# A bidirectional encoder layer on one core: the four later conditioning rows, from TensorE matmuls in one sweep to VectorE sums over two

## The chip, the cores and the metric

One core of one Trainium2 chip runs the whole kernel in one launch. The metric is the device time of that launch in microseconds (us), taken from its first to its last instruction with what the launch itself adds; lower is better. Before the change the median of three runs is 2424.1 us (2421.89 to 2425.3).

The core has five instruction streams that run beside each other and wait for each other by semaphores: PE (TensorE, matmuls, with its weight loads shown apart as PEld), DVE (VectorE), ACT (ScalarE), POOL (GpSimd) and SP (SyncE, which here issues nearly all DMA transfers). [...]

## The reference

One layer of an encoder (D_MODEL = 1024), run for a prompt of 2048 rows and for a sample of 256 rows, each with a conditioning vector `c` of its own. Cut to what matters here:

```python
def encoder_layer(x, c, ...):
    mod = silu(c) @ ada_w + ada_b                       # (1024) @ (1024 x 6144)
    sh1, sc1, gt1, sh2, sc2, gt2 = split(mod, 6)        # six rows of 1024
    h = rmsnorm(x, norm_mix) * (1 + sc1) + sh1
    x = x + gt1 * hybrid_mixer(h, w_in, w_fnet, w_out)  # FNet half and retention half
    h = rmsnorm(x, norm_mlp) * (1 + sc2) + sh2
    x = x + gt2 * (square(relu(h @ w_mlp_in)) @ w_mlp_out)
    return x
```

`mod` has one row for each of the two sequences. `sh1` and `sc1` are wanted before the first projection; `gt1`, `sh2`, `sc2` and `gt2`, the later rows of the title, are wanted only behind the mixer, in the output projection and the MLP.

## The kernel before, in words

The 2304 rows are 18 tiles of 128 rows (16 prompt, 2 sample). The program has these stages: a start in which `ada0` makes `sh1` and `sc1`; a pass over all tiles that projects the Fourier part and forms the first butterflies on DVE (to about 165 us); the **first sweep** over the tiles from the last to the first, which makes keys and values (`w_k`, `w_v`) and the backward retention states, and runs the rest of the Fourier transform (`dft`, `pa`, `pb`, `fs`) in small jobs between (about 165 to 470 us); the **second sweep** in forward order, which makes queries and the gate (`w_q`, `w_g`), and the retention itself (about 470 to 775 us); then the output projection and the MLP, the other two thirds of the time.

Matrices are multiplied in float32r as three products of a high and a low part, so each projection of one tile is 24 matmuls 128x512 (`proj<-whi,hhi`, `proj<-wlo,hhi`, `proj<-whi,hlo`, eight each). The matmuls of the conditioning rows are plain float32, and the profile shows each of them as two records, one for each pass.

The order of instructions on every engine is fixed when the program is built: a scheduler plays the program through on a timeline of its own and writes each engine's list. Tiles come from pools of a fixed number of slots, and an instruction that makes a new tile waits until a slot is free. Those that matter here: `S` has 13 slots of 128x1024 float32 (inputs `h`, their parts `hhi` and `hlo`, `kv`, `qkT`, the weights `raw`, and the conditioning weights `ada`), `H` has 4 of 128x512, and PSUM pool `PC` has two banks.

**The later conditioning rows before.** There are two blocks (`bt` = 1 and 2) of 2048 columns of `ada_w`: block 1 holds `gt1` and `sh2`, block 2 `sc2` and `gt2`. `ada_begin(bt)` writes the bias into a PSUM bank: four matmuls with 12 rows of contraction and 32 columns of weights, one for each 512 columns of the block, each into its own 32 partitions (`ada<-boot,ident`). Then each of 16 steps of the first sweep (n = 1 to 16) takes one of eight slices `k` of the contraction: `ada_load` fetches two tiles 128x1024 of `ada_w` and `ada_step` adds four matmuls with 128 rows and 32 columns of weights (`ada<-ada,boot`), whose stationary operand is a 32-column slice of silu(c) and of which two columns are of use. `ada_end` copies the bank out (ACT), stores the gate row to DRAM and transposes the row that becomes a scale or shift in `aff`.

**The second sweep's step.** `retention` does, on PE, the transposes of `kv`, `q` and of the tile before (`tr`), the state product `kvf`, the scores `sc`, and then the output `o`. Of `o`, one matmul for each head takes the scores after DVE multiplied them by the decay (`qkT<-sc,dec`, L771). On DVE stand `qx` (two), `sfn` (four), `hlo`, `qkT` and the split of a `w_out` piece (`wolo`).

## Time and profile before

| | |
|---|---|
| median of three runs | 2424.1 us (2421.89 to 2425.3) |
| the profiled execution | 2425.7 us, span 2423.8 us |
| TensorE clock granted, mean over the span | 0.986 |
| PE, DVE, ACT, POOL busy over the span | 97%, 61%, 41%, 5% |
| moved by DMA | 411.62 MB, 170 GB/s mean |

The profiled execution is 1.6 us above the median, so differences can be read from it as they stand. "Busy" counts the modelled length of matmuls, which overlap each other: two matmuls that start 0.23 us apart are listed with 0.39 us each. The cost of a matmul is therefore read from when the next one starts, not from its listed length. A row of the timeline gives start, length, engine, line, operation, and out<-in, with equal neighbours merged (`x8`: eight records).

### The profile page before, as it was taken

To read this page: it belongs to the slowest core of one execution; us is meant where nothing else is said; L and a number is where in the kernel's file an instruction comes from. 1 tells how busy PE (TensorE), PEld (TensorE's weight loads), DVE (VectorE), ACT (ScalarE), POOL (GpSimd) and SP (SyncE) were. 2 spreads that over 40 slices of the span, in tenths; PEclk is the share of its full clock that TensorE was granted. 3 is DMA by queue.
4 is the path that set the end of the run, shared out by engine and by line. 5 is a ranking of instruction groups with operands and counts; after the bars stand their busy time and mean duration, and the time that the engine had idled before them with its cause. 6 is when DMAs were issued, how large, how long until landed. Compare 5 with 4: busy or idle time off the path is not lost.

```text
span 2423.8 us, 30933 instructions
## 1 busy us (share of the span) xinstructions
PE 2351.3 (97%) x11985; PEld 2042.4 (84%) x11985; DVE 1466.8 (61%) x2188; ACT 1003.7 (41%) x1684; POOL 113.2 (5%) x191
## 2 busy tenths in 40 slices
PE   7999999999999999999999999998899999999998
PEld 4777787788887888899999999998688788788786
DVE  3574544334534754655685578556746867867887
ACT  4752222123333543555665566555434323323332
POOL 0101000001111000000000000000000000000000
PEclk8999999999999999999999999999899999999999
DMA  7547649324333455533453345433433545545774
GB/s 278 214 152 269 208 153 330 138 71 137 122 104 116 144 165 187 177 124 123 158 185 122 122 159 190 135 122 124 168 124 132 203 173 191 191 156 221 259 276 168
DMA packets 183771, 411.62 MB, mean 170 GB/s; under 512 B 12052, under 2 KB 80436, under 8 KB 176712
## 3 DMA queue, kind: packets, MB, share of 16 engines
q1 hardware_dynamic: 182040, 405.58, 48.5%
q0 software_dynamic: 1584, 4.06, 0.6%
q8 instruction: 94, 1.54, 0.3%
q14 instruction: 53, 0.43, 0.1%
HBM read 274.05 MB, written 135.54 MB: 169 GB/s over the span
## 4 chain that ended last, share of the span: by engine, by line
PE 54%; DVE 3%; DMA 1%; ACT 0%; issue 0%; POOL 0%; DVEq 0%; POOLq 0%; ACTq 0%
PE mX L964 31%; PE mZ L964 15%; PE mY L964 8%; DVE woB L81 1%; DVE woT L81 1%; DMA hr<-hidd 1%; DVE ho L81 0%; DVE acc L1181 0%; DVE o L242 0%; DVE t L242 0%; DVE hr L242 0%; DMA o<-w_mlp_out 0%; ACT ho L80 0%; ACT woT L80 0%; ACT woB L80 0%
## 5 line engine op out<-in xcount | busy, mean ns | idle before, releaser
L964 PE MATMUL mX<-woT,ho 128*128 128x512 f32 x1296 | 312.1, 390 | 1.3 <-ACT x L1127 1.3
L80 ACT CAST ho<-hr 128x512 fp32r<-128x512 f32 x252 | 152.7, 621 | 346.9 <-PE mX L964 219.3
L964 PEld LDWEIGHTS mX<-woT,ho 128*128 128x128 f32 x1296 | 243.9, 188 | 53.2 <-issue 1.7
L964 PE MATMUL mX<-opS,wT 128*128 128x384 f32 x1152 | 208.2, 334 | 0.0
L84 PE MATMUL proj<-whi,hhi 128*128 128x512 f32 x720 | 194.1, 407 | 13.3 <-ACT hhi L80 7.8
L964 PEld LDWEIGHTS mX<-opS,wT 128*128 128x128 f32 x1152 | 200.5, 188 | 0.0
L81 DVE TENSOR_TENSOR ho<-hr,ho 128x512 fp32r<-128x512 f32 x252 | 169.6, 686 | 33.3 <-ACT ho L80 32.9
L84 PE MATMUL proj<-wlo,hhi 128*128 128x512 f32 x720 | 185.4, 394 | 0.0
L84 PE MATMUL proj<-whi,hlo 128*128 128x512 f32 x720 | 182.6, 392 | 0.0
L84 PEld LDWEIGHTS proj<-whi,hhi 128*128 128x128 f32 x720 | 134.1, 193 | 53.0 <-issue 10.9
L84 PEld LDWEIGHTS proj<-wlo,hhi 128*128 128x128 f32 x720 | 134.5, 189 | 31.8 <-issue 4.2
L84 PEld LDWEIGHTS proj<-whi,hlo 128*128 128x128 f32 x720 | 134.0, 188 | 30.5 <-issue 3.4
L81 DVE TENSOR_TENSOR wB<-mr,wB 128x1024 fp32r<-128x1024 f32 x72 | 87.9, 1221 | 86.7 <-ACT wB L80 86.5
L964 PE MATMUL mX<-woB,ho 128*128 128x512 f32 x432 | 113.5, 398 | 13.6 <-ACT woB L80 9.6
L964 PE MATMUL mZ<-woT,ho 128*128 128x512 f32 x432 | 109.8, 396 | 14.9 <-ACT woT L80 10.4
L1181 DVE TENSOR_TENSOR acc<-mX,acc 128x512 f32<-128x512 f32 x117 | 79.8, 687 | 73.0 <-PE mX L964 66.2
L964 PE MATMUL mY<-woB,ho 128*128 128x512 f32 x432 | 114.8, 399 | 0.0
L964 PEld LDWEIGHTS mX<-woB,ho 128*128 128x128 f32 x432 | 82.1, 191 | 34.8 <-ACT woB L80 11.8
L964 PEld LDWEIGHTS mZ<-woT,ho 128*128 128x128 f32 x432 | 82.0, 190 | 34.0 <-ACT woT L80 11.7
L964 PE MATMUL mY<-opA,wB 128*128 128x384 f32 x576 | 106.7, 339 | 2.4 <-DVE x L159 2.4
L102 POOL TENSOR_SCALAR rv<-ss 128x1 f32<-128x1 f32 (+1 forms) x72 | 18.2, 252 | 1900.2 <-ACT x L145 1408.9
L80 ACT CAST wB<-mr 128x1024 fp32r<-128x1024 f32 x72 | 75.3, 1046 | 76.1 <-PE mY L964 41.0
(243 smaller groups left out, 4331.2 us busy)
## 6 DMA issues: line engine op xcount, KB each, us to landing
mr<-w_mlp_in SPq DMA_DIRECT2D x96, 512.0 KB, 4.1
hidd<-hid SPq DMA_DIRECT2D x48, 768.0 KB, 3.8
hr<-hidd SPq DMA_DIRECT2D x27, 1024.0 KB, 6.3
accd<-acc SPq DMA_DIRECT2D x27, 1024.0 KB, 4.7
acc<-accd SPq DMA_DIRECT2D x27, 1024.0 KB, 4.9
ada<-ada_w SPq DMA_DIRECT2D x48, 512.0 KB, 6.5
h<-hd SPq DMA_DIRECT2D x36, 512.0 KB, 4.2
x<-x_prompt SPq DMA_DIRECT2D x32, 512.0 KB, 4.9
```

Of the source, the lines that this page charges most:

```text
L80: act.copy(hi, src)
L81: dve.tensor_tensor(out=lo, in0=src, in1=hi.bitcast(F32), op=ALU.subtract)
L84: pe.matmul(out, l, r, start=first, stop=last)
L102: pool.tensor_scalar(out=v[:, :n], in0=ss[:, :n], scalar1=scale, scalar2=EPS, op0=ALU.mult, op1=ALU.add)
L964: pe.matmul(out, l, r, start=first and fresh, stop=last, skip_group_check=not fresh)
L1181: dve.tensor_tensor(out=acc[:, b_], in0=o, in1=acc[:, b_], op=ALU.add)
```

## The change

The later rows are cut into four pieces `pc` of 1024 columns (`gt1`, `sh2`, `sc2`, `gt2`), and each piece into eight slices `k`. For one slice, `ada_piece` loads one tile 128x1024 and lets DVE do two operations 128x1024, one for each sequence: the tile times the per-partition scalar silu(c) (from the new tile `c2`), for k > 0 plus the running sum `adacc`. After the eighth slice `ada_end` adds over partitions on PE: for each of four groups (two sequences, two halves of the columns) a bias matmul (12 rows) and then a matmul of a 128x32 tile of ones with the sum. The bias is loaded anew into a tile `br`. Copy, gate rows and transposes follow as before, on four pieces and not on two blocks.

There are 32 slices. Seventeen are done in the first sweep (n = 1 to 17), the other fifteen in the second (n = 0 to 14). So two of the four ends, those of `gt1` and `sh2`, lie in the first sweep, and those of `sc2` and `gt2` in the second.

```diff
+    ones = cp.tile([P, 32], F32, name="ones")
+    dve.memset(ones, 1.0)
+    c2 = cp.tile([P, KD, 4], F32, name="c2")
...
-    def ada_step(m, k, tiles):
-        for j in range(4):
-            mm(m[32 * j:32 * j + 32, :], cT[:, k, :],
-               tiles[j // 2][:, (j % 2) * 512:(j % 2) * 512 + 512], False, k == KD - 1)
...
+    def ada_piece(pc, k):
+        w = t4("ada", "S")
+        c0 = 2048 + pc * 1024
+        sp.dma_start(out=w, in_=ada_view[:, k, c0:c0 + 1024])
+        for s_ in range(2):
+            if k == 0:
+                acc_[s_] = t4("adacc", "S")
+                dve.tensor_scalar(out=acc_[s_], in0=w, scalar1=c2[:, k, s_:s_ + 1], scalar2=None, op0=ALU.mult)
+            else:
+                dve.scalar_tensor_tensor(out=acc_[s_], in0=w, scalar=c2[:, k, s_:s_ + 1], in1=acc_[s_],
+                                         op0=ALU.mult, op1=ALU.add)
+        if k == KD - 1:
+            ada_end(pc)
+
+    def ada_end(pc):
+        br = t2("br", "H")
+        sp.dma_start(out=br[0:12, :], in_=a["ada_b"].rearrange("o (r c) -> (o r) c", c=512))
         m = tps("ada", "PC")
...
+        for g in range(4):
+            s_, hf = divmod(g, 2)
+            r = 4 + 2 * pc + hf
+            o = m[32 * g:32 * g + 32, :]
+            mm(o, ident[0:12, r:r + 1].to_broadcast([12, 32]), br[0:12, :], True, False)
+            mm(o, ones, acc_[s_][:, hf * 512:hf * 512 + 512], False, True)
         s = t2("adas", "H")
         act.copy(s, m)
...
-        if n >= 1 and ada_jobs:
-            bt, k = ada_jobs.pop(0)
-            if k == 0:
-                ada_m[bt] = ada_begin(bt)
-            ada_step(ada_m[bt], k, ada_load(bt, k, "S"))
-            if k == KD - 1:
-                ada_end(bt, ada_m[bt])
+        if n >= 1:
+            ada_piece(*ada_jobs.pop(0))
...
         pend = (t, kv, s_b, q, sg)
+        if ada_jobs:
+            ada_piece(*ada_jobs.pop(0))
```

The new tiles move instructions on every engine from the first sweep on; ahead of about 180 us the order is the same. Three places matter.

**PE, first sweep, eighth slice.** In the list before, around the last slice of block 1 (`ada_2674` and `ada_2676` are the two weight tiles, `boot_103` holds silu(c), `dft` and `proj` are Fourier and projection matmuls):

```order
L84 MATMUL dft_2609<-tab_2588,zl_2593 128x256
L84 MATMUL ada_1600<-ada_2674,boot_103 32x512 x2
L84 MATMUL proj_2694<-whi_924,hhi_2442 128x512
L84 MATMUL ada_1600<-ada_2676,boot_103 32x512 x2
L84 MATMUL proj_2694<-whi_930,hhi_2442 128x512 x2
```

The end of the first piece in the list after, at the same step (`br` is the bias tile, `adacc_1606` and `adacc_1608` the sums of the two sequences):

```order
L84 MATMUL dft_2760<-tab_2752,zl_2757 128x256
L84 MATMUL ada_2653<-br_2651,ident 32x512
L84 MATMUL ada_2653<-adacc_1606,ones 32x512
L84 MATMUL ada_2653<-br_2651,ident 32x512
L84 MATMUL ada_2653<-adacc_1606,ones 32x512
L84 MATMUL ada_2653<-br_2651,ident 32x512
L84 MATMUL ada_2653<-adacc_1608,ones 32x512
L84 MATMUL ada_2653<-br_2651,ident 32x512
L84 MATMUL ada_2653<-adacc_1608,ones 32x512
L84 MATMUL dft_2760<-tab_2752,zh_2756 128x256 x2
```

What stood as pairs between projections at each of 16 steps is gone from there, and four times there stand eight matmuls in one row, in which 12 rows of contraction and 128 rows take turns.

**DVE, second sweep, one step.** Before, from the second `qx` to the split of a `w_out` piece (`wolo`; `hlo` is the low part of the next tile's input):

```order
L765 TENSOR_TENSOR qx_4598<-tr_4592,xi_3804 128x512
L245 SCALAR_TENSOR_TENSOR sfn_4627<-sfn_4482,kvf_4622 128x128 x4
L81 TENSOR_TENSOR hlo_4706<-h_4558,hhi_4705 128x1024
L771 TENSOR_TENSOR qkT_4585<-sc_4601,dec_3802 128x512
L81 TENSOR_TENSOR wolo_4698<-raw_4695,wohi_4697 128x1024
```

After, in the step of that tile, which holds the eighth slice of the third piece:

```order
L757 TENSOR_TENSOR qx_4577<-tr_4571,xi_3759 128x512
L239 SCALAR_TENSOR_TENSOR sfn_4606<-sfn_4457,kvf_4601 128x128 x4
L81 TENSOR_TENSOR hlo_4709<-h_4537,hhi_4708 128x1024
L356 SCALAR_TENSOR_TENSOR adacc_3693<-ada_4674,c_101,adacc_3693 128x1024
L763 TENSOR_TENSOR qkT_4564<-sc_4580,dec_3757 128x512
L356 SCALAR_TENSOR_TENSOR adacc_3695<-ada_4674,c_101,adacc_3695 128x1024
L81 TENSOR_TENSOR wolo_4701<-raw_4698,wohi_4700 128x1024
```

One of the two sums has come in ahead of `qkT`; in most other steps of the second sweep both stand ahead of it, then mostly with `hlo` behind.

**PE, second sweep, the same step.** Before, from the state product on (`o<-kv,qkT`, which needs the DVE result above, stands behind all 24 matmuls of `proj_4923`):

```order
L84 MATMUL kvf_4622<-vz_4620,kv_4411 128x128 x4
L84 MATMUL sc_4601<-qkT_4585 128x128 x4
L84 MATMUL o_4607<-sfn_4482,qx_4598 128x128
L84 MATMUL o_4607<-q_4513,qx_4598 128x128
L84 MATMUL proj_4923<-whi_3323,hhi_4705 128x512 x2
L84 MATMUL proj_4923<-whi_3329,hhi_4705 128x512 x2
```

After:

```order
L84 MATMUL kvf_4601<-vz_4599,kv_4386 128x128 x4
L84 MATMUL sc_4580<-qkT_4564 128x128 x4
L84 MATMUL o_4586<-sfn_4457,qx_4577 128x128
L84 MATMUL o_4586<-q_4488,qx_4577 128x128
L84 MATMUL o_4586<-kv_4386,qkT_4564 128x128
L84 MATMUL o_4586<-sfn_4457,qx_4577 128x128
```

At the two ends in the second sweep the rest of `o` and then the eight matmuls of `ada_end` come ahead of the projection. In five of the other steps two thirds of a projection (16 matmuls) stand between `sc` and `o<-kv,qkT`, and the last third behind; in the rest the place is as before.

## The prediction

> **What bounds the kernel now.** I read the page's busy shares first, then a table of windows for the two sweeps that the change touches, then who waited for whom in them, and last PE's timeline around the instructions that go.

> ```profile
> PE 2351.3 (97%) x11985; PEld 2042.4 (84%) x11985; DVE 1466.8 (61%) x2188; ACT 1003.7 (41%) x1684; POOL 113.2 (5%) x191
> 163.00:470.00 307.00, 307.00 (x1597) 239.06 (x1596) 149.24 (x287) 74.73 (x104) 25.99 (x29) 1.00 0.64 224
> 470.00:775.00 305.00, 297.97 (x1705) 256.50 (x1703) 125.30 (x245) 96.03 (x258) 36.75 (x46) 1.00 0.32 108
> ```

> The window rows give stretch, length, then busy time and count of PE, PEld, DVE, ACT and POOL, the granted clock, the DMA share and GB/s. In the first sweep PE is listed busy all 307.00 us at full clock, in the second 297.97 of 305.00. So in the first sweep a microsecond less on PE is a microsecond less in all, as long as DVE (149 of 307) keeps up. In the second there are 7 us of waiting, and most of it has one name:

> ```profile
> PE proj L84 <- ACT sg L864: 5.6, 12, 0.5
> PE o L84 <- DVE qkT L771: 0.6, 1, 0.6
> ```

> Twelve waits of about half a microsecond for a ScalarE result, and one of 0.6 us for the DVE product `qkT` (line, releaser, us in total, times, longest). Behind the sweeps nothing of the change remains but loads of the gates, which are there under either plan.

> **What goes: 16 steps and two bias rows on PE.** All records of the removed matmuls in the first sweep, 128 of weights and 16 of bias (two to a matmul), and the timeline around three of their bursts:

> ```profile
> L84 PE MATMUL ada<-ada,boot x128: 592/605/617, 187.1 to 435.4; 128*32 128x512 f32 x128
> L84 PE MATMUL ada<-boot,ident x16: 587/600/612, 186.1 to 324.9; 12*32 12x512 f32 x16
> 186.07 1.06 PE L84 MATMUL ada<-boot,ident 12*32 12x512 f32 x8
> 187.06 1.06 PE L84 MATMUL ada<-ada,boot 128*32 128x512 f32 x8
> 188.06 0.50 PE L84 MATMUL proj<-wlo,hhi 128*128 128x512 f32 x1
> 188.39 2.00 PE L84 MATMUL proj<-whi,hlo 128*128 128x512 f32 x8
> 190.23 0.39 PE L84 MATMUL proj<-whi,hhi 128*128 128x512 f32 x1
> 190.55 1.05 PE L84 MATMUL ada<-ada,boot 128*32 128x512 f32 x4
> 191.53 1.89 PE L84 MATMUL proj<-whi,hhi 128*128 128x512 f32 x7
> 193.25 1.07 PE L84 MATMUL proj<-wlo,hhi 128*128 128x512 f32 x4
> 281.01 0.28 PE L84 MATMUL pb<-yl,mh 128*128 128x256 f32 x1
> 281.13 0.28 PE L84 MATMUL pb<-yh,ml 128*128 128x256 f32 x1
> 281.34 1.04 PE L84 MATMUL ada<-ada,boot 128*32 128x512 f32 x2
> 282.31 0.50 PE L84 MATMUL dft<-tab,zh 128*128 128x256 f32 x2
> 282.65 0.28 PE L84 MATMUL dft<-tab,zl 128*128 128x256 f32 x1
> 434.90 1.05 PE L84 MATMUL ada<-ada,boot 128*32 128x512 f32 x4
> ```

> The listed lengths are no price, since matmuls into different quarters of the columns run side by side; starts are. Eight projection matmuls take 190.23 - 188.39 = 1.84 us. The eight that enclose the burst at 190.55 take 193.25 - 190.23 = 3.02 us, so two matmuls (x4) cost 1.18 us. The lone matmul at 281.34 (x2) stands among three small ones that are 0.12 us apart: 282.65 - 281.13 = 1.52, less 0.36, is 1.16 us. And four together (x8) occupy 188.06 - 187.06 = 1.00 us. One, two or four cost the same. So bursts are to be counted, not matmuls: from the one at 187.06 to that at 434.90 there are 27 (five of x8, twenty of x4, one of x6, one of x2; together 128 records). They cost 27 x 1.17 = 31.6 us. Each of the two bias rows ahead of a first burst adds 187.06 - 186.07 = 0.99 us. **Removed: 33.6 us of PE**, in a stretch where PE has nothing to wait for.

> **What comes on PE: four ends of eight matmuls.** This is the term on which the sign hangs. The bias has 12 rows of contraction and the ones have 128, and they take turns. The trace shows what PE does when the shape changes:

> ```profile
> PEld proj L84 <- issue: 18.4, 22, 0.8
> PEld ada L84 <- issue: 6.8, 17, 0.8
> ```

> Weight loads, which elsewhere run ahead of the matmuls, stand idle about 0.8 us at each change to or from these shapes in the first sweep, with nothing named that they wait for: the next shape's weights are loaded only when the last matmul of the shape before is through. From 12 to 128 rows that holds as well: the bias row of 186.07 is followed by the next shape 0.99 us later, as long as a burst takes before a full-width matmul. So I take each of the eight as a burst of its own: a lone matmul lasts 282.31 - 281.34 = 0.97 us to the next shape, the bias 0.99, in the mean 0.98. One end is 8 x 0.98, plus 1.17 - 0.98 = 0.19 for getting in and out, so 8.0 us. **Added: 4 x 8.0 = 32.1 us** (from 4 x 8.03). The lower bound is two bursts to an end, 2 x 0.98 + 0.19 = 2.15, 8.6 us for four. I take the upper one because the row nearest to it, bias followed by weights, is of these two shapes. PE alone then comes to 32.1 - 33.6 = -1.5 us: nearly the whole saving is given back.

> [...]

> **What comes on DVE: 64 operations.** Their prices are those of the same operations on tiles of that size:

> ```profile
> L176 DVE TENSOR_SCALAR x<-x,rr 128x1024 f32<-128x1024 f32 x18 | 13.5, 752 | 15.8 <-POOL rr L105 15.7
> L1118 DVE SCALAR_TENSOR_TENSOR acc<-acc,rr,nf 128x1024 f32<-128x1024 f32 x16 | 20.5, 1280 | 4.2 <-POOL rr L105 4.2
> ```

> Eight at 0.75 us and 56 at 1.28 us (mean ns of one is the second number behind the bar) are 78 us. Of these 34 operations, about 41 us, lie in the first sweep, where DVE then is at 190 of some 290 us. I cost them at nothing there: PE's cover is the 24 matmuls (3 x 1.84 = 5.5 us) of each projection, and a pair takes 2.5 us. That cover is thinnest where the Fourier butterflies still fill DVE, before about 191 us; 0 to +3 us, taken as 0. The other 30 lie in the second sweep, and there they stand ahead of a product that PE waits for. One step of it:

> ```profile
> 607.60 0.69 DVE L763 TENSOR_TENSOR qx<-tr,xi 128x512 f32<-128x512 f32 x1 [3.11 <-ACT qkT L760]
> 608.18 1.06 PE L84 MATMUL sc<-qkT 128*128 128x128 f32 x8
> 608.20 0.68 DVE L765 TENSOR_TENSOR qx<-tr,xi 128x512 f32<-128x512 f32 x1
> 608.80 0.87 DVE L245 SCALAR_TENSOR_TENSOR sfn<-sfn,kvf 128x128 f32<-128x128 f32 x4
> 609.30 0.39 PE L84 MATMUL o<-q,qx 128*128 128x128 f32 x2
> 609.45 2.08 PE L84 MATMUL proj<-whi,hhi 128*128 128x512 f32 x8
> 609.59 1.22 DVE L81 TENSOR_TENSOR hlo<-h,hhi 128x1024 fp32r<-128x1024 f32 x1
> 610.73 0.68 DVE L771 TENSOR_TENSOR qkT<-sc,dec 128x512 f32<-128x512 f32 x1
> ```

> Now the order of the change is laid over these times. **At the two ends** `o<-kv,qkT` follows the scores with no projection between, so PE is ready at about 609.5. `qkT` stands behind `hlo` and one sum: `hlo` from 609.59 to 610.73, the sum 1.2 us to 611.9, `qkT` to 612.6. PE waits 3.1 us, twice: +6.2 us. It would be 1.9 if the sum were through ahead of `hlo`, and 3.7 if a POOL operation stretched it by 0.55 (below). **In the other steps** a pair runs from 609.67 (end of `sfn`) to 612.1 and `qkT` to 612.8. Where two thirds of the projection stand between, PE wants it at 609.3 + 2 x 1.84 = 613.0, and `hlo`, now behind, ten small matmuls later (about 614.1) for the last third, which is just when it is done. The slack is 0.1 to 0.2 us, so I take 0.6 us for each of the five steps of that order, +3.0. There, on the other hand, the half microsecond of waiting for ScalarE should go, since eight matmuls are left over to cover it: five of the twelve, -2.3. Together +0.7; bounds -5.6 (all twelve go) and +15 (1 us in each of 15 steps).

> DVE and POOL get in each other's way:

> ```profile
> 292.55 1.53 POOL L719 TENSOR_TENSOR vz<-kv,zc 128x512 f32<-128x512 f32 x1 [10.24 <-issue]
> 293.39 1.77 DVE L81 TENSOR_TENSOR hlo<-h,hhi 128x1024 fp32r<-128x1024 f32 x1 [0.21 <-ACT hhi L80]
> ```

> Beside a POOL operation a DVE operation with two inputs took 1.77 us and not 1.22. Where that hits a pair it costs 0.55 us, which is the 0.6 above. [...]

> **Transfers.** Fifteen loads of 512 KB move into the second sweep; SP issues each in about 0.4 us ahead of the loads of `raw`, `kv` and `h`.

> ```profile
> 601.59 0.43 SPq L653 DMA_DIRECT2D h<-hd  x1
> 607.92 1.07 ACT L80 CAST hhi<-h 128x1024 fp32r<-128x1024 f32 x1
> h<-hd SPq DMA_DIRECT2D x36, 512.0 KB, 4.2
> ```

> `h` lands at about 605.8 and is used at 607.9, so 0.4 us later costs nothing. That cover is gone if the load finds no free slot of `S`, of which the two sums now hold two throughout: then SP stands, and `kv` and `h` behind it. DMA share is 0.32 there, so bandwidth is no issue. The first sweep's 32 loads become 17. The new bias loads, copies and gate stores, four ends for two, lie beside the projections and cost nothing.

> **The sum**, against the profiled execution: 2425.7 - 33.6 + 32.1 + 6.2 + 0.7 = 2431.1, which is +5.4 us. The median of the runs shown is 2424.1, so 2430.

> **The rivals.**
> - *The quarters run side by side* although shapes alternate: 8.6 us for four ends and not 32.1. For it: four matmuls of one shape take 1.00 us. Against it: each change of shape in the trace stalls the weight loads. 2430 - 23.5 = 2406, a clear gain. Should each ones matmul overlap the next bias, five slots to an end (4 x 5.1 = 20.4) give 2418. [...]
> - *DVE becomes the pace of the second sweep.* Were each of the 15 steps 1 us late, through POOL, a missing slot of `S` or a late `h`, that would be +15 for +0.7: 2444. It begins beyond 0.1 to 0.2 us of delay a step, the slack worked out above. Against it: DVE is at 125 of 305 us, and 37 more still leave it under 55%.
> - *The stall at the two ends is not there and the ScalarE waits all go*: -1.5 - 5.6 gives 2417 at best. It is the low edge of my own case.

> **Chances.** Serial ends as summed: 0.58, with a range of its own from 2420 to 2438. Side by side 0.14, half overlapped 0.08, DVE as the pace 0.20. A measurement of this kernel tells about 0.2% (4.8 us) from no change. My case lies just above that line: 0.32 of its 0.58 slower, 0.21 the same, 0.05 faster. Side by side is faster, half overlapped is split between faster and the same, DVE as the pace is slower. That gives 0.24 faster, 0.24 the same, 0.52 slower. The range that leaves out 2 in 10 goes from the first rival's 2406 to 2442.

> **What would show it.** In the changed kernel's PE timeline the eight matmuls of an end (two records each) should start about 0.98 us apart (8 us in all); if they start a few nanoseconds apart, the first rival holds. The first sweep should be about 33.6 - 16.1 = 17.5 us shorter with PE still at 100%. In the second, waits of PE for `qkT` should come to 6 us in two long ones; many short ones, or waits for `hlo`, would speak for the second rival. The prediction is wrong if the granted clock falls during the narrow matmuls, of which no row here tells.

## The result, and the profile after

The changed kernel takes 2446.2 us (median of five runs, 2434.5 to 2450.3) against 2424.1 us before: a ratio of 1.0084 with a 95% interval of 1.0065 to 1.0103. It is slower, as the likelier side of the prediction had it, but by 22 us and not by 6, and outside the range of 2406 to 2442. The profiled execution after took 2443.8 us (span 2441.8), 18.1 more than the one before; the readings below account for these 18 us.

The windows of the two sweeps after (stretch, length, then busy time and count of PE, PEld, DVE, ACT and POOL, granted clock, DMA share, GB/s):

```profile
163.00:470.00 307.00, 305.55 (x1569) 251.42 (x1568) 195.95 (x332) 76.00 (x113) 31.43 (x31) 1.00 0.61 203
470.00:775.00 305.00, 291.47 (x1550) 233.57 (x1549) 149.90 (x256) 90.04 (x235) 37.31 (x44) 0.96 0.37 120
```

DVE went up as foreseen (149 to 196 and 125 to 150 us), and PE lost 6.5 us of busy time in the second stretch. What nobody had asked for stands in the last columns: the granted clock of the second stretch is 0.96 and not 1.00. Since the sweeps have shifted, the second is better cut from its first scores to its last. Before, then after:

```profile
472.60:779.00 306.40, 297.10 (x1705) 255.66 (x1703) 125.38 (x248) 96.83 (x261) 37.95 (x48) 1.00 0.32 107
```

```profile
453.40:796.20 342.80, 326.42 (x1742) 263.14 (x1740) 162.22 (x277) 100.20 (x265) 39.74 (x48) 0.96 0.35 116
```

So the second sweep starts 472.6 - 453.4 = 19.2 us earlier and lasts 342.8 - 306.4 = 36.4 us longer; 0.9 us more come behind it. That is the whole difference: -19.2 + 36.4 + 0.9 = +18.1.

An end in the first sweep, on PE's timeline, is as predicted: eight matmuls 0.97 us apart, 313.47 - 305.69 = 7.8 us.

```profile
305.69 1.04 PE L84 MATMUL ada<-br,ident 12*32 12x512 f32 x2
306.66 1.04 PE L84 MATMUL ada<-adacc,ones 128*32 128x512 f32 x2
...
312.50 1.04 PE L84 MATMUL ada<-adacc,ones 128*32 128x512 f32 x2
313.47 0.50 PE L84 MATMUL dft<-tab,zh 128*128 128x256 f32 x2
```

The first end of the second sweep is not:

```profile
554.95 0.39 PE L84 MATMUL o<-q,qx 128*128 128x128 f32 x2
559.09 0.79 PE L84 MATMUL o<-kv,qkT 128*128 128x128 f32 x2 [3.75 <-DVE qkT L763]
559.67 0.64 PE L84 MATMUL o<-sfn,qx 128*128 128x128 f32 x2
...
563.65 1.91 PE L84 MATMUL ada<-br,ident 12*32 12x512 f32 x2
565.49 1.92 PE L84 MATMUL ada<-adacc,ones 128*32 128x512 f32 x2
...
576.55 1.92 PE L84 MATMUL ada<-adacc,ones 128*32 128x512 f32 x2
578.40 3.64 PE L84 MATMUL proj<-whi,hhi 128*128 128x512 f32 x8
581.87 2.00 PE L84 MATMUL proj<-wlo,hhi 128*128 128x512 f32 x8
```

PE waits 3.75 us for `qkT`, and what follows runs at half speed: pairs of `o` 0.43 us apart (0.22 at full clock), the eight narrow matmuls 1.84 us apart, 578.40 - 563.65 = 14.75 us for 7.8, and still the first eight of the projection take 3.47 us for 1.84. Windows laid exactly on the two stretches in which the trace's clock reads a half, at the third end and at the fourth:

```profile
557.80:581.70 23.90, 22.61 (x44) 8.41 (x45) 6.68 (x11) 3.42 (x12) 1.20 (x2) 0.50 0.14 39
725.10:728.50 3.40, 3.40 (x18) 3.32 (x16) 0.76 (x2) 0.17 (x1) 0.00 (x0) 0.50 0.00 0
```

PE was busy 22.6 and 3.4 us in them; at full clock the same work takes about half (7.8 for 14.75, 1.84 for 3.47), so some 26.0 / 2 = 13.0 us of the 36.4 are the clock. Before, no stretch of the sweeps was at half clock.

At the fourth end the wait was just as long, but the clock was full again before the narrow matmuls began, and they ran 0.97 us apart (728.61 to 736.39):

```profile
724.55 0.49 PE L84 MATMUL o<-kv,qkT 128*128 128x128 f32 x2 [3.75 <-DVE qkT L763]
...
728.61 1.04 PE L84 MATMUL ada<-br,ident 12*32 12x512 f32 x2
```

What differs is where the clock changed. In the trace its changes lie whole multiples of 3.413 us apart: the two falls 725.10 - 557.80 = 167.3 us, 49 of them, and the stretches are seven and one of them long. Call such a piece of 3.413 us a clock window. At the third end the clock fell with 1.3 us of the wait still to come; the first clock window at half clock was idle in part, and the second, from 561.25 us on, held narrow matmuls from 563.65. At the fourth end it fell 0.55 us after the wait was over, and `o` alone filled the one clock window up to 728.5. Where the clock windows lie in the program is not fixed: the first fall stands 25.88 us behind the start of the span in the trace before and 25.36 us in the one after, although the order of the instructions is the same there. That it is luck which end pays is the author's estimate from this.

### The profile page after: what moved, and what is told of

It reads as the page before. It is cut to its first block, busy times and chain, and to the rows that moved or that the text cites. A ratio compares the mean times of both kernels' runs of the same rounds, so it can differ in the third digit from the quotient of the medians.

```text
span 2441.8 us, 30876 instructions
## 1 busy us (share of the span) xinstructions
PE 2357.6 (97%) x11905; PEld 2043.2 (84%) x11905; DVE 1545.1 (63%) x2254; ACT 1006.3 (41%) x1686; POOL 118.9 (5%) x191
## 3 DMA queue, kind: packets, MB, share of 16 engines
q8 instruction: 93, 1.52, 0.3%
## 4 chain that ended last, share of the span: by engine, by line
PE 54%; DVE 3%; DMA 1%; issue 0%; ACT 0%; POOL 0%; DVEq 0%; POOLq 0%; ACTq 0%
PE mX L958 31%; PE mZ L958 15%; PE mY L958 8%; DVE woB L81 1%; DVE woT L81 1%; DMA hr<-hidd 1%; DVE ho L81 0%; DVE acc L1175 0%; DVE o L236 0%; DVE t L236 0%; DMA o<-w_mlp_out 0%; DVE hr L236 0%; DVE hs L236 0%; ACT woT L80 0%; DVE acc L1128 0%
## 5 line engine op out<-in xcount | busy, mean ns | idle before, releaser
L80 ACT CAST ho<-hr 128x512 fp32r<-128x512 f32 x252 | 152.6, 621 | 347.3 <-PE mX L958 216.2
L84 PE MATMUL proj<-whi,hhi 128*128 128x512 f32 x720 | 190.6, 402 | 9.2 <-ACT hhi L80 7.8
L81 DVE TENSOR_TENSOR ho<-hr,ho 128x512 fp32r<-128x512 f32 x252 | 169.5, 686 | 31.5 <-ACT ho L80 30.9
L84 PE MATMUL proj<-wlo,hhi 128*128 128x512 f32 x720 | 186.6, 397 | 0.0
L84 PE MATMUL proj<-whi,hlo 128*128 128x512 f32 x720 | 183.5, 393 | 0.9 <-DVE hlo L81 0.9
L84 PEld LDWEIGHTS proj<-whi,hhi 128*128 128x128 f32 x720 | 133.8, 191 | 39.4 <-ACT hhi L80 8.7
L84 PEld LDWEIGHTS proj<-wlo,hhi 128*128 128x128 f32 x720 | 136.2, 192 | 28.1
L84 PEld LDWEIGHTS proj<-whi,hlo 128*128 128x128 f32 x720 | 133.2, 188 | 28.5 <-DVE hlo L81 1.1
L81 DVE TENSOR_TENSOR wB<-mr,wB 128x1024 fp32r<-128x1024 f32 x72 | 87.9, 1221 | 85.9 <-ACT wB L80 85.9
L958 PE MATMUL mX<-woB,ho 128*128 128x512 f32 x432 | 113.2, 397 | 14.4 <-ACT woB L80 10.1
L105 POOL TENSOR_SCALAR rv<-ss 128x1 f32<-128x1 f32 (+1 forms) x72 | 18.2, 253 | 1905.7 <-ACT x L139 1409.6
L80 ACT CAST wB<-mr 128x1024 fp32r<-128x1024 f32 x72 | 75.3, 1046 | 76.4 <-PE mY L958 41.0
## 6 DMA issues: line engine op xcount, KB each, us to landing
mr<-w_mlp_in SPq DMA_DIRECT2D x96, 512.0 KB
ada<-ada_w SPq DMA_DIRECT2D x48, 512.0 KB
h<-hd SPq DMA_DIRECT2D x36, 512.0 KB
x<-x_prompt SPq DMA_DIRECT2D x32, 512.0 KB
```

Source lines behind the costliest of these rows:

```text
L80: act.copy(hi, src)
L81: dve.tensor_tensor(out=lo, in0=src, in1=hi.bitcast(F32), op=ALU.subtract)
L84: pe.matmul(out, l, r, start=first, stop=last)
L105: pool.tensor_scalar(out=v[:, :n], in0=ss[:, :n], scalar1=scale, scalar2=EPS, op0=ALU.mult, op1=ALU.add)
L958: pe.matmul(out, l, r, start=first and fresh, stop=last, skip_group_check=not fresh)
```

## The experiments

Two explanations of the missing 13 us stood against each other. **A:** the wait for `qkT` halves the clock, and a row of narrow matmuls of alternating shape does not raise it again, so the half clock lasts as long as they do. **B:** the clock is an aside; the alternating shapes, or the 30 sums on DVE in the second sweep, cost that much by themselves. The kernel before ran beside each group of experiments (medians 2424.2 to 2424.3 us).

**grouped: the shape changes once in an end.**

```diff
-        for g in range(4):
-            ... bias of g, then ones of g
+        for g in range(4):
+            mm(<quarter g>, ident[0:12, r:r + 1]..., br[0:12, :], True, False)
+        for g in range(4):
+            mm(<quarter g>, ones, acc_[s_][:, ...], False, True)
```

> Edit: the same eight matmuls of each end, but the four with 12 rows of bias first and the four with 128 rows of ones behind, so that the shape changes once in an end and not seven times. Theory A (what my sum lacked is the clock: at the third end the wait for `qkT` halves the granted clock and the slow serial matmuls behind it keep it halved for 24 us): an end falls from 8.0 to about 2.2 us, 4 x 5.9 = 23.5 us less, and the half-clock stretch at the third end shrinks from 24 to under 12 us because the full projection comes sooner, another 6 us: 2446 - 23.5 - 6 = 2416 us (2412 to 2420). Theory B (the clock is not it, the alternating shapes and late `qkT` are all): 2446 - 23.5 = 2423 us, and the half-clock stretch keeps its length. If the time of an end does not come from the change of shape: 2446, eight starts 0.97 us apart.

Measured: 2416.9 us (2411.0 to 2417.7), ratio 0.9963 (0.9950 to 0.9975). The timeline of the third end, and the window on its half-clock stretch:

```profile
546.26 0.49 PE L84 MATMUL o<-kv,qkT 128*128 128x128 f32 x2 [2.97 <-DVE qkT L763]
...
550.12 1.21 PE L84 MATMUL ada<-br,ident 12*32 12x512 f32 x8
551.26 1.06 PE L84 MATMUL ada<-adacc,ones 128*32 128x512 f32 x8
552.25 2.11 PE L84 MATMUL proj<-whi,hhi 128*128 128x512 f32 x8
```

```profile
547.10:550.50 3.40, 3.40 (x19) 2.99 (x22) 2.31 (x3) 0.70 (x2) 0.00 (x0) 0.50 0.02 5
```

The four quarters of one shape (x8) run side by side, an end takes 2.1 us, and half clock lasts 3.4 us although the wait of 3 us is still there. 29 us faster than the changed kernel: more than the 23.5 of the shapes alone, as A had it. The short stretch by itself does not prove A, since `o` filled most of that clock window and the narrow matmuls reach only 0.35 us into it.

**oneshape: the order stays, the bias gets 128 rows.** The twelve rows of `br` are extended by zeros, so bias and ones have one shape, in the program still in turns.

```diff
+        dve.memset(br, 0.0)
...
-            mm(o, ident[0:12, r:r + 1].to_broadcast([12, 32]), br[0:12, :], True, False)
+            mm(o, ident[:, r:r + 1].to_broadcast([P, 32]), br, True, False)
```

> Edit: the order of the eight matmuls stays bias, ones, bias, ones, but the bias matmul gets 128 rows of contraction too (the rows behind the twelve are set to zero and the weights are zero there), so that all eight have one shape. If the change of shape is what serialises an end: the two of one quarter of the columns follow each other and the next quarter's run beside them; an end takes 2 to 5 us for 8.0, so 12 to 24 us less by that and 3 to 6 us less at half clock: 2416 to 2431 us. If two matmuls into the same quarter serialise whatever their shape, with no overlap between the quarters: still about 0.97 us apart, 2446 us.

Measured: 2409.7 us (2407.0 to 2411.8), ratio 0.9942 (0.9928 to 0.9955), 6 us below the low end of its forecast; why it gained that much is not shown. The first end:

```profile
305.01 1.08 PE L84 MATMUL ada<-br,ident 128*32 128x512 f32 x8
305.90 1.06 PE L84 MATMUL ada<-adacc,ones 128*32 128x512 f32 x8
306.89 0.50 PE L84 MATMUL dft<-tab,zh 128*128 128x256 f32 x2
```

In the program bias and ones of one quarter follow each other; on the chip the four quarters start within 0.04 us (x8 lasts 1.08 us where one matmul, x2, lasts 1.04), the biases at 305.01 us and the ones at 305.90, and the eight take 306.89 - 305.01 = 1.9 us. So neither the alternation nor two matmuls into the same quarter serialised this end, only the change of shape did: 7.8 us with seven changes, 1.9 with none.

**firstsweep: all 32 slices in the first sweep, serial ends.**

```diff
         if n >= 1:
-            ada_piece(*ada_jobs.pop(0))
+            for _ in range(2):
+                if ada_jobs:
+                    ada_piece(*ada_jobs.pop(0))
```

> Edit: two slices instead of one at each step of the first sweep, so that all 32 slices and all four serial ends lie in the first sweep and the second has none. Theory A (loss in the second sweep: wait for `qkT`, half clock): serial ends stay at 4 x 8.03 = 32.1 against 33.6 removed, nothing is left in the second sweep, its waits for ScalarE come back: 2424 - 1.5 + 0 to 3 for thinner cover on VectorE = 2423 to 2426 us, no half-clock stretch in either sweep. Rival (64 sums on VectorE are the pace wherever they stand, 149 + 78 = 227 us of 295 in the first sweep): waits of TensorE for VectorE in the first sweep of 10 us or more, 2433 us or above.

Measured: 2429.5 us (2427.6 to 2432.7), ratio 1.0024 (1.0015 to 1.0033). No half-clock stretch in either sweep (granted clock 1.00 from 163 to 470 us and from 470 to 775), although four times narrow matmuls run in turns: narrow serial work alone did not halve a full clock here. It is 3.5 us above the top of A's forecast and 3.5 below the rival's; PE's waits in the first sweep are 3.0 us, not 10:

```profile
PE dft L84 <- ACT zh L80: 1.7, 1, 1.7
PE fs L84 <- DVE yl L81: 1.3, 2, 1.1
```

The rest was not followed further: the fourth end is divided among projection matmuls there, with more changes of shape than one end has.

**bankPB: another PSUM bank for the third and fourth end.** In the changed kernel `ada` takes one of the two banks of `PC`, which `sc` and `o` need in turn; so `o` had to be finished ahead of the end, with no projection to cover the wait for `qkT`. A bank of `PB` takes that away.

```diff
-        m = tps("ada", "PC")
+        m = tps("ada", "PC" if pc < 2 else "PB")
```

> Edit: the PSUM bank of the third and fourth end comes from pool PB (three banks, transposes and state products) and not from PC (two banks, which the scores and the output `o` take in turn). Everything else is the same, 15 slices in the second sweep included. In the built order the projection stands again between the scores and `o<-kv,qkT` in nearly all steps, with the end's matmuls divided around `o`. Theory A: without the 3.75 us waits for `qkT` the clock stays full; the ends cost 8 us each and some shape changes against `o` more: 2424 - 33.6 + 32.1 + 1 = 2424 us, up to 2429. Rival (30 sums on VectorE are the pace of the second sweep, whatever the order on TensorE): waits for `qkT` spread over the steps, 2436 us or above. Second rival (the serial narrow matmuls by themselves halve the clock): a half-clock stretch of over 10 us at the third or fourth end, 2432 us or above.

Measured: 2438.1 us (2434.9 to 2442.5), ratio 1.0059 (1.0046 to 1.0071). A missed by 9 us, and in its numbers the second rival came out: a half-clock stretch of over 10 us and more than 2432. Of the first rival only the time fits, not the place: the steps between the two ends are as before the change (scores start at 605.4, 623.1, 640.7 and on to 711.5 us, 17.7 apart), with all 15 slices still in this sweep. So the sums on DVE cost nothing there, and the rival of the DVE pace is out. Both ends, however, have a wait again, now for the sum itself, and half-clock stretches of 10.2 and 6.8 us:

```profile
PE ada L84 <- DVE adacc L356: 3.2, 2, 2.0
```

```profile
715.39 1.05 PE L84 MATMUL ada<-adacc,ones 128*32 128x512 f32 x2 [1.21 <-DVE adacc L356]
716.37 1.04 PE L84 MATMUL ada<-br,ident 12*32 12x512 f32 x2
717.34 1.87 PE L84 MATMUL ada<-adacc,ones 128*32 128x512 f32 x2
719.14 1.91 PE L84 MATMUL ada<-br,ident 12*32 12x512 f32 x2
```

At the third end the wait was 1.99 us; at the fourth a wait of only 1.21 us stands there, with narrow matmuls around it. Either the narrow matmuls by themselves lower the clock, as the second rival had it, or a short wait among them is enough. The next two kernels were to separate the wait from the narrow work. (A third stretch of 3.4 us at half clock lies in the first sweep, at 236.15 us, with no narrow matmul near: PE had waited 1.23 us for `zh` and 0.53 for `zl` in the clock window before it, 1.76 together. In the changed kernel these waits are 0.92 and 0.53, 1.45 together, and the clock stayed full.)

**fillPB: the wait of bankPB filled with wide matmuls.** In this kernel and in fill_behind sixteen matmuls 128x512 stand at the head of each of these two ends and write the same bank; the next matmuls overwrite it (`hl_[0]` is the input of the step's projections).

```diff
+        if pc >= 2:
+            for i in range(16):
+                mm(m, hl_[0][0][:, 0:128], hl_[0][0][:, 512:1024], i == 0, i == 15)
         for g in range(4):
```

> Edit: the kernel with the bank from PB (2438 us), and ahead of the third and fourth end sixteen more wide matmuls into that bank (128x512, their result is overwritten, so they add work and nothing else). They fill the 2.0 us in which TensorE there waits for the sum `adacc`. Theory A (a wait of two or more microseconds halves the clock, and serial narrow matmuls behind it do not lift it): no half-clock stretch at the third and fourth end, where the kernel without the filling has 10.2 and 6.8 us; the filling costs 2 x (3.7 - 2.0) = 3.4 us and the clock gives back 17 / 2 = 8.5 us: 2433 us in spite of 32 matmuls more. Rival (the narrow matmuls between `o` halve the clock, wait or no wait): the half-clock stretches stay, 2438 + 3.4 = 2441 us or more.

Measured: 2431.1 us (2428.5 to 2434.5), ratio 1.0028 (1.0017 to 1.0040): 7 us faster than bankPB with 32 matmuls more. From the scores to the end of the narrow ones PE is never idle and the clock is full, at the third end (the row below) and at the fourth:

```profile
555.00:570.30 15.30, 15.30 (x66) 7.68 (x64) 8.98 (x13) 2.81 (x4) 1.04 (x1) 1.00 0.19 58
```

The narrow matmuls stand around `o` as in bankPB; without the wait they did not lower the clock (1.00 in the row). So the second rival is out too, and A's trigger is widened: waits of 2.0 and of 1.21 us were enough. The narrow matmuls about the shorter one seem to have counted, since in these traces no clock window without such matmuls lowered the clock with less than 1.6 us of idling (last section).

**fill_behind: the wait stays, wide matmuls stand behind it.** The same sixteen, in the changed kernel with its `PC` bank, where they come after `o` and so after the wait.

> Edit: the changed kernel as it is (bank from PC, serial shapes, third and fourth end behind `o`), with sixteen more wide matmuls between `o` and the eight narrow ones of these two ends; their result is overwritten. The wait of 3 to 3.75 us for `qkT` stays, since the filling stands behind it. Theory A (the wait halves the clock, wide work lifts it again, serial narrow work does not): the half-clock stretch at the third end is 3.4 to 10 us instead of 23.9 and over before the narrow matmuls, which start 0.97 us apart at both ends; 10 us come back from the clock, 2 x 3.7 to 7.4 us go into the filling: 2440 to 2447 us, about as before the filling. Rival (the narrow serial matmuls hold the clock down whatever stands ahead of them): the stretch runs through them, 1.84 us apart, 24 us or more at half clock, 2451 us or above.

Measured: 2435.7 us (2433.4 to 2439.6), ratio 1.0049 (1.0037 to 1.0062), 10.6 us faster than the same kernel without the 32 matmuls (1.0065 to 1.0103). The third end:

```profile
558.77 0.67 PE L84 MATMUL o<-kv,qkT 128*128 128x128 f32 x2 [3.75 <-DVE qkT L767]
...
562.65 3.91 PE L84 MATMUL ada<-hhi 128*128 128x512 f32 x16
566.50 1.04 PE L84 MATMUL ada<-br,ident 12*32 12x512 f32 x2
567.47 1.04 PE L84 MATMUL ada<-adacc,ones 128*32 128x512 f32 x2
```

```profile
558.90:562.30 3.40, 3.40 (x17) 3.40 (x18) 2.14 (x2) 0.00 (x0) 0.00 (x0) 0.50 0.00 0
```

The wait is the same 3.75 us, the half clock now lasts 3.4 us instead of 23.9, and the eight narrow matmuls keep 0.97 us, so the rival is out. But in this execution the wide matmuls did not end the half clock: it ran from 558.93 to 562.35 us and the first of them starts at 562.65; at the fourth end it ran from 715.95 to 719.36, and they start at 719.87. At both ends `o` had filled the clock window before them. Over the whole span of five executions each, the clock took 29 to 39 us here and 37 to 51 in the changed kernel (span times what the mean clock lacks to 1), which fits A, but the profile does not show the filling at work. The time came out below the forecast partly because the built order changed too: six steps between the ends are back at 17.7 us from 17.8 to 19.0, 2.5 us in all.

**thin: what the removed matmuls cost.** The kernel before, its loads kept:

```diff
-            ada_step(ada_m[bt], k, ada_load(bt, k, "S"))
+            tl = ada_load(bt, k, "S")
+            if k in (0, KD - 1):
+                ada_step(ada_m[bt], k, tl)
```

> Edit: the kernel before, with the matmuls of twelve of its sixteen first-sweep steps left out (k = 1 to 6 of both blocks; their loads stay, the conditioning rows lack these slices). It prices what the change removes: 27 bursts x 12/16 = 20.3 bursts at 1.17 us = 23.7 us, so 2400.6 us (2398 to 2403). If the first sweep is held by anything beside TensorE, or the bursts hide in part: less is gained, 2408 or above.

Measured: 2400.2 us (2395.8 to 2401.7), 24.0 below 2424.2 where 23.7 were expected. A burst cost 24.0 / 20.3 = 1.18 us, and the first sweep had no other bound down to there.

**first_oneshape and oneshape_PB: two combinations.** The edits are those above, joined.

> Edit: all 32 slices in the first sweep (two at a step) and bias matmuls of 128 rows, so that an end has one shape and none lies in the second sweep. If the parts add up: 2429.5 - 4 x (7.8 - 1.9) = 2406 us (2402 to 2409), second sweep as in the kernel before, no half-clock stretch in the sweeps. If VectorE is the pace of the first sweep once TensorE is shorter there: waits for `zl` or `yl` grow and it stays at 2412 or above.

Measured: 2416.7 us (2414.2 to 2420.8), ratio 0.9971 (0.9960 to 0.9981), a miss by 10 us. The time is the rival's, but of its sign little shows: PE waits 2.1 us for `yl`. Two slices at a step, and TensorE no longer held by serial ends, expose another wait; the transposes of an end wait for the copy of its bank:

```profile
PE adat L381 <- ACT adas L373: 4.5, 1, 4.5
```

and a half-clock stretch of 6.8 us lies right on it (383.3 us). ACT's list has three casts `whi<-raw` ahead of that copy, and the first of them had waited 12.86 us for the load `raw<-w_in`; the copy started at 383.68, behind the last.

> Edit: bias matmuls of 128 rows and the bank of the third and fourth end from PB. Sums stay in both sweeps. Against the one-shape kernel (2409.7): the steps of the second sweep go back from 18.0 to 17.7 us (8 of them, -2.4), the two waits of 3.0 us for `qkT` become two of about 2.0 for the sum, but the ends are divided around `o`, some 2 us of shape changes more for both: 2407 us (2403 to 2412). If the rearranged order of the second sweep cost more than the waits show: 2400 or less.

Measured: 2410.8 us (2406.0 to 2413.5), ratio 0.9944 (0.9932 to 0.9957), within the forecast and level with oneshape. Waits for the sum are 1.2 us at either end, here with no half clock; the narrow matmuls behind them run side by side.

**deferPB: the third and fourth end one step later.** One shape, bank from `PB`, and `ada_end` called one step after the last slice, when its sums are long done.

```diff
-        if k == KD - 1:
+        if k == KD - 1 and pc < 2:
             ada_end(pc)
+        elif k == KD - 1:
+            owed.append(pc)
...
         pg = proj(hl, w_g)
+        if owed:
+            ada_end(owed.pop(0))
```

> Edit: one shape, bank from PB, and the third and fourth end are put into the program one step later, when the sums have long been through. In the built order an end then stands in one piece between the scores and `o`, and nothing of it waits. Both theories agree on the mechanism, the run asks for the best version: against one shape and bank from PB (2410.7, where each of the two ends still lengthened its step by 6 us through the wait for the sum and the parting around `o`) an end now costs 2.0 us and the matmuls of `o` find `qkT` done: 2 x 4 us less, 2403 us (2399 to 2407), no half-clock stretch in the sweeps. If the remaining 6 us were not the wait and the parting: 2410 again.

Measured: 2400.5 us (2397.6 to 2401.4), ratio 0.9898 (0.9883 to 0.9914). An end is one piece, nothing of it waits, and `qkT` is done when `o` asks for it:

```profile
560.62 1.08 PE L84 MATMUL ada<-br,ident 128*32 128x512 f32 x8
561.50 1.06 PE L84 MATMUL ada<-adacc,ones 128*32 128x512 f32 x8
562.50 0.49 PE L84 MATMUL o<-sfn,qx 128*128 128x128 f32 x2
562.82 0.39 PE L84 MATMUL o<-q,qx 128*128 128x128 f32 x2
563.10 0.49 PE L84 MATMUL o<-kv,qkT 128*128 128x128 f32 x2
```

This is the best version, 1.0% below the kernel before, and it agrees with the sum of the parts: 2424.2 - 33.6 + 4 x 2.1 = 2399.0.

## Why the prediction was wrong

**Removed, 33.6 us of PE: right.** thin measured 24.0 for 23.7 of it.

**Serial ends, 4 x 8.0 us: right.** The eight starts lie 0.97 us apart, and the lower bound of about 2 us is what one shape gives (oneshape). One row was misread on the way: the weight loads of `ada` stood idle 0.4 us in the mean (6.8 in 17), not 0.8; no term hangs on it.

**First sweep 17.5 us shorter: right within 2 us.** It is 19.2 us in the profiles, but about 2 of them arose ahead of any change. The same projection, behind the same wait, before and after:

```profile
131.85 3.36 PE L84 MATMUL proj<-whi,hhi 128*128 128x512 f32 x7 [2.14 <-ACT hhi L80]
```

```profile
129.69 2.50 PE L84 MATMUL proj<-whi,hhi 128*128 128x512 f32 x8 [2.14 <-ACT hhi L80]
```

**The stall at the two ends, 2 x 3.1 us: the size nearly right, its consequence missed.** Both waits were 3.75 us, the prediction's upper case of 3.7 with a POOL operation beside the sum:

```profile
555.24 1.22 DVE L81 TENSOR_TENSOR hlo<-h,hhi 128x1024 fp32r<-128x1024 f32 x1
556.37 2.06 DVE L356 SCALAR_TENSOR_TENSOR adacc<-ada,c,adacc 128x1024 f32<-128x1024 f32 x1
558.35 0.68 DVE L763 TENSOR_TENSOR qkT<-sc,dec 128x512 f32<-128x512 f32 x1
```

The step that failed is the price of this wait. The prediction counted a wait of 3.1 us as 3.1 us. It cost the wait and then what ran at half clock behind it: some 13.0 us in the profiled execution, nearly all at the one end whose narrow matmuls it caught. The second sweep was to grow by 2 x 8.03 + 6.2 + 0.7 = 23.0 us; it grew by 36.4, and 36.4 - 13.0 = 23.4. So the clock is all but the whole miss. The prediction did name the clock as what would make it wrong, but gave that case no chance and no place in the range, and it named the wrong trigger: in firstsweep and fillPB the narrow matmuls left a full clock at 1.00. At the third end they did not raise a half one in 14.75 us, and after the first clock window of wide ones (578.4 to 581.7 us) it was full.

The half-clock stretches in the sweeps lasted 3.4, 6.8, 10.2 and 23.9 us: one, two, three and seven clock windows. A whole one of idling was not needed for a fall: before the one at 557.8 PE had been idle for 2.5 us of the clock window, and in bankPB 1.76, 1.99 and 1.21 us were enough.

**Other steps, +0.7 us: 2 us too low, and not by the waits it counted.** Five waits for `qkT` of 0.46 to 0.60 us came, 2.8 us where 3.0 were taken (of the nine in the row below two are the ends', and two, 1.1 us together, are in the kernel before too), and nine waits for ScalarE went and not five:

```profile
PE o L84 <- DVE qkT L763: 11.4, 9, 3.8
PE proj L84 <- ACT sg L856: 1.4, 3, 0.5
```

Yet the seven steps between the ends took 17.8 to 19.0 us for 17.7, 2.9 us more in all, while PE's waits in them add up to 4.2 us for 3.2; the rest stands in no wait. bankPB puts this down to the order on PE, and through it to the two banks of `PC`: with the end in another pool the sums are the same and the steps are 17.7 us.

**The rivals.** Side by side did not happen here; with one shape it did (oneshape, 1.9 us for an end). DVE as the pace is refuted by bankPB, though its 2444 us is nearest to the result: that is luck. Many short waits for `qkT`, its sign, came only as the five already in the sum.

**The median.** The other executions vary with the clock: 2434.5 us at a mean granted clock of 0.985, 2450.3 at 0.979. 0.006 of 2440 us is 15 us, nearly the whole spread of 16. So the clock decides not only the mean but how far the runs lie apart; with that taken off (span times mean clock) the five lie at 2396 to 2400 us against 2387 to 2394 in the runs of the kernel before, some 7 us more in the middle, near the 5.4 of the sum.

## What to carry to other kernels

A wait of TensorE of a few microseconds is not to be priced by its length alone: look at what runs behind it, because small matmuls of alternating shape can stand in a stretch at half clock from the first to the last (14.75 us of 23.9 here). In the same execution this happened at one end and not at the other, so read several. Small reductions on TensorE should have one shape throughout (pad the contraction with zeros), which here made an end 1.9 us instead of 7.8, and stand where their inputs have long been ready. A temporary that borrows a PSUM bank from a chain of two rearranges that chain; ask which pool it takes from before asking what it computes.

## What the runs showed of the hardware

The two POOL rows of that comparison, of the changed kernel and of grouped:

```profile
555.96 1.39 POOL L779 TENSOR_TENSOR vz<-kv,zc 128x512 f32<-128x512 f32 x1 [6.99 <-DMA mixd<-rT]
```

```profile
544.48 2.02 POOL L779 TENSOR_TENSOR vz<-kv,zc 128x512 f32<-128x512 f32 x1 [7.56 <-DMA mixd<-rT]
```

In the changed kernel the sum took 0.78 us longer than in grouped; in grouped `vz` took 0.98 us longer than alone.
